# A long convolution by half-size cosine and sine transforms at odd frequencies, in place of full-size ones

## The chip, the cores and the metric

The kernel runs as one program on one core of a Trainium2 chip. The metric is the device time of one execution in microseconds. Five engines take part: TensorE (PE, with its weight loads as PEld), VectorE (DVE), ScalarE (ACT), GpSimd (POOL), and SyncE (SP), whose queue issues the transfers. An instruction waits in its engine's queue until all that it reads and all that it overwrites is ready.

## The reference, cut to what matters

The program is four transformer blocks on 512 tokens of width 1024 with 256 context tokens. The second block's mixer has a long convolution over 512 channels, applied twice, each time followed by a gate:

```python
def two_sided(h_fwd, h_bwd):
    return jnp.concatenate([h_fwd, jnp.zeros((1, h_fwd.shape[1]), h_fwd.dtype), h_bwd[:0:-1]], axis=0)

def fft_long_conv(u, filt2, skip):
    length = u.shape[1]
    n = 2 * length
    y = jnp.fft.irfft(jnp.fft.rfft(u, n=n, axis=1) * jnp.fft.rfft(filt2, n=n, axis=0), n=n, axis=1)[:, :length]
    return y + u * skip.astype(F32)
...
    filt = hyena_filters(length, w1, b1, freq1, w2, b2, freq2, w3)
    z = v
    for order, gate in enumerate((x1, x2)):
        z = gate * fft_long_conv(z, two_sided(filt[:, order, 0], filt[:, order, 1]), skip[order])
```

`hyena_filters` makes the filters from a small network over the 512 positions, times a decay, divided by the sum of their magnitudes. The filters depend on weights alone.

## The kernel before

Every large product is done in split precision: an operand is a rounded high half and the rest, and `mm3` issues three matmuls per tile (lines 90, 91, 92: high x high, data low, weight low). `wsplit` brings a weight tile of 128x512 or 128x1024 by SP's queue, makes its high half on ScalarE (L73, `whi`) and its low half on VectorE (L74, `wlo`); two of each are held. `split` does the same with data (L84, L85). A 128x512 piece of a transform with four tiles of contraction is 12 matmuls of 128x512.

The work of the convolution lies at two places.

The spectra of the two filters are made in the first block's mixer, `even_mixer`. `hyena_spectra` is a generator that `even_mixer` draws on (`next(fg)`) between its own products. The sums and differences of the two filter directions, four tiles each, are split, and the spectrum is made in nine pieces of 128 frequencies x 512 channels (five cosine pieces from the sums, four sine pieces from the differences), each by 12 matmuls with its own 128x512 weight tile. A piece is scaled on VectorE (L713, by the reciprocal norm `hyinv`), the cosine pieces get the skip weight on GpSimd (L715), and SP stores it (L759) from one of two buffers `hyspec`. In the same mixer VectorE does the 31-tap convolution of another branch, 28 taps for each of four channel tiles and two token ranges: 224 instructions of L450. Its gated q, k and v products and the attention follow.

The convolution itself is in the second block's mixer, `odd_mixer`. There the gated delta rule runs in steps (`Delta.step`: `prep`, with a small triangular solve of seven rounds on VectorE at L1183 to L1187, then `recur`), and then `finish`. Each calls `fill()` at its waits, which draws on a generator: first `rows()` (the projections, short convolutions and transposes of the branch, four tiles of v and eight of the gates, steps 2 to 4), then `hyena()`. For each order `hyena` does four frequency tiles: cosine and sine piece (24 matmuls, two weight tiles of 128x512), product with the stored spectrum (`hysp`, L1005, L1006 on VectorE, L1007 on GpSimd), split. Then four token tiles of the inverse, 24 matmuls each with a weight tile of 128x1024, and the gate's multiply (L1022), whose result is split again for the second order. At the end 16 transposes (L1029) bring the result to channels by tokens for the od_w_out product.

The Tile framework's scheduler sets the order on each engine from the order of the program and its pools; each engine then runs its list in order.

## Time and profile before

| | |
|---|---|
| three runs, us | 3699.78, 3704.36, 3707.05 (median 3704.36) |
| profiled execution, us | 3703.5, its span 3701.7 |
| TensorE busy, matmuls | 3475.7 us (94%), 22228 |
| VectorE busy | 2448.4 us (66%) |
| ScalarE, GpSimd busy | 1474.4 us (40%), 683.1 us (18%) |
| DMA | 377.22 MB, mean 102 GB/s |

The profile is that of one execution, on the same core. Busy time is the time in which an engine had an instruction running; matmuls overlap their neighbours, so that the spacing of their starts, and not the duration of one, is what a matmul costs in a row of them. The window view gives busy time per stretch, with the number of instructions in brackets, then the granted TensorE clock as a share of full speed (PEclk), the share of busy DMA engines and the bandwidth. The tile view groups a tile's instructions by line. The timeline view lists single instructions in order of start.

### The profile page before, as it was taken

How to read it: one execution, taken by the hardware profiler on the slowest of the kernel's cores; microseconds unless marked ns; L12 is line 12 of the kernel's file. 1: busy time of each engine (PE TensorE's matmuls, PEld its weight loads, DVE VectorE, ACT ScalarE, POOL GpSimd, SP SyncE). 2: the span in 40 equal slices, each digit the busy share in tenths (PEclk: the TensorE clock that was granted, in tenths of full speed). 3: DMA queues.
4: the chain of work that ended last, by engine and by line, in shares of the span. 5: the costliest groups of instructions: out<-in, count | busy, mean ns of one | idle time of the engine just before them, and what ended most of it. 6: DMA issues, size and time to landing. Idle time of an engine off the chain costs nothing.

```text
span 3701.7 us, 55774 instructions
## 1 busy us (share of the span) xinstructions
PE 3475.7 (94%) x22228; PEld 2869.9 (78%) x22228; DVE 2448.4 (66%) x4099; ACT 1474.4 (40%) x2541; POOL 683.1 (18%) x601
## 2 busy tenths in 40 slices
PE   6898999999998899989999989999999999999999
PEld 4666777888887667667888777767998777767998
DVE  7998877544458765554333776567887676657886
ACT  4213643213226444333223445453443544643443
POOL 0133201002102432221111032022111032011110
PEclk9998999999999999999999989999999999999999
DMA  5244113343333222332232322332333313232333
GB/s 199 80 159 131 49 49 119 115 125 120 119 105 115 84 76 83 120 126 81 91 97 91 111 60 92 108 111 78 105 103 94 122 51 114 80 127 76 106 102 98
DMA packets 161165, 377.22 MB, mean 102 GB/s; under 512 B 19687, under 2 KB 44647, under 8 KB 160520
## 3 DMA queue, kind: packets, MB, share of 16 engines
q1 hardware_dynamic: 160904, 373.65, 32.1%
q8 instruction: 174, 2.85, 0.3%
q14 instruction: 87, 0.71, 0.1%
HBM read 341.61 MB, written 28.84 MB: 100 GB/s over the span
## 4 chain that ended last, share of the span: by engine, by line
PE 40%; DVE 13%; issue 7%; ACT 4%; POOL 2%; DMA 2%; SPq 0%; DVEq 0%; ACTq 0%; POOLq 0%
PE acc L90 11%; PE acc L92 11%; PE acc L91 11%; DVE wlo L74 2%; DMA wraw<-in_w_up_dram 1%; DVE wslo L85 1%; ACT whi L73 1%; DVE hb L1576 1%; PE rec L1301 1%; PE rec L1302 1%; PE rec L1286 1%; DVE ws L1884 1%; DVE xl L1987 1%; DVE oz L819 1%; ACT mp L1811 0%
## 5 line engine op out<-in xcount | busy, mean ns | idle before, releaser
L73 ACT CAST whi<-wraw 128x1024 fp32r<-128x1024 f32 (+2 forms) x468 | 424.0, 906 | 917.9 <-PE acc L91 729.8
L74 DVE TENSOR_TENSOR wlo<-wraw,whi 128x1024 fp32r<-128x1024 f32 (+2 forms) x464 | 511.4, 1103 | 186.0 <-ACT whi L73 181.5
L90 PE MATMUL acc<-hh,whi 128*128 128x512 f32 (+1 forms) x1024 | 366.5, 358 | 11.7 <-ACT whi L73 8.5
L92 PE MATMUL acc<-hh,wlo 128*128 128x512 f32 (+1 forms) x1024 | 363.4, 356 | 10.2 <-POOL wlo L74 5.8
L91 PE MATMUL acc<-hl,whi 128*128 128x512 f32 (+1 forms) x1024 | 364.3, 356 | 1.2 <-DVE hl L256 0.8
L91 PE MATMUL acc<-hidl,whi 128*128 128x512 f32 (+1 forms) x768 | 275.0, 358 | 3.0 <-DVE hidl L85 3.0
L90 PE MATMUL acc<-hidh,whi 128*128 128x512 f32 (+1 forms) x768 | 275.0, 358 | 0.0
L92 PE MATMUL acc<-hidh,wlo 128*128 128x512 f32 (+1 forms) x768 | 274.8, 358 | 0.0
L341 POOL TENSOR_TENSOR sqr<-relu 128x512 f32<-128x512 f32 (+1 forms) x96 | 127.4, 1328 | 688.5 <-ACT relu L339 684.1
L90 PEld LDWEIGHTS acc<-hh,whi 128*128 128x128 f32 x1024 | 195.0, 190 | 51.9 <-ACT whi L73 13.5
L92 PEld LDWEIGHTS acc<-hh,wlo 128*128 128x128 f32 x1024 | 194.0, 190 | 43.9 <-DVE wlo L74 7.7
L91 PEld LDWEIGHTS acc<-hl,whi 128*128 128x128 f32 x1024 | 195.7, 191 | 33.3 <-DVE hl L256 3.5
L92 PE MATMUL acc<-shh,wlo 128*128 128x512 f32 (+1 forms) x480 | 193.7, 404 | 6.7 <-DVE wlo L74 6.7
L90 PE MATMUL acc<-shh,whi 128*128 128x512 f32 (+1 forms) x480 | 195.7, 408 | 3.5 <-ACT whi L73 3.5
L91 PE MATMUL acc<-shl,whi 128*128 128x512 f32 (+1 forms) x480 | 194.2, 405 | 0.0
L85 POOL TENSOR_TENSOR flo<-fth,fhi 128x512 fp32r<-128x512 f32 x44 | 83.7, 1903 | 532.6 <-ACT fhi L84 491.0
L90 PE MATMUL acc<-fsh,wshi 128*128 128x256 f32 x576 | 164.2, 285 | 4.5 <-ACT wshi L84 4.5
L91 PEld LDWEIGHTS acc<-hidl,whi 128*128 128x128 f32 x768 | 145.9, 190 | 26.7 <-DVE hidl L85 3.4
L91 PE MATMUL acc<-fsl,wshi 128*128 128x256 f32 x576 | 163.9, 285 | 0.0
L191 DVE SCALAR_TENSOR_TENSOR mdacc<-wraw,cs,mdacc 128x1024 f32<-128x1024 f32 x70 | 94.4, 1372 | 104.6 <-DMA wraw<-in_ada_w_dram 104.4
L92 PE MATMUL acc<-fsh,wslo 128*128 128x256 f32 x576 | 162.4, 285 | 0.7 <-DVE wslo L85 0.7
L90 PEld LDWEIGHTS acc<-hidh,whi 128*128 128x128 f32 x768 | 144.9, 189 | 23.3
(671 smaller groups left out, 9305.3 us busy)
## 6 DMA issues: line engine op xcount, KB each, us to landing
wraw<-in_mlp_w_dram SPq DMA_DIRECT2D x128, 512.0 KB, 3.5
wraw<-in_ada_w_dram SPq DMA_DIRECT2D x96, 512.0 KB, 4.0
wraw<-in_w_in_dram SPq DMA_DIRECT2D x58, 512.0 KB, 3.5
wraw<-in_od_w_fm_dram SPq DMA_DIRECT2D x36, 512.0 KB, 3.5
wraw<-in_w_gate_dram SPq DMA_DIRECT2D x72, 256.0 KB, 3.2
wraw<-in_w_up_dram SPq DMA_DIRECT2D x72, 256.0 KB, 3.2
wraw<-in_w_down_dram SPq DMA_DIRECT2D x48, 256.0 KB, 2.7
wraw<-in_w_down_dram SPq DMA_DIRECT2D x32, 320.0 KB, 2.9
```

The costliest lines, as they stand in the source:

```text
L73: nc.scalar.copy(hi, raw)
L74: (eng or nc.vector).tensor_tensor(out=lo, in0=raw, in1=f32(hi), op=ALU.subtract)
L85: (eng or nc.vector).tensor_tensor(out=lo, in0=src, in1=f32(hi), op=ALU.subtract)
L90: nc.tensor.matmul(out, s[0], m[0], start=first, stop=False)
L91: nc.tensor.matmul(out, s[0], m[1], start=False, stop=False)
L92: nc.tensor.matmul(out, s[1], m[0], start=False, stop=last)
L191: nc.vector.scalar_tensor_tensor(out=acc, in0=w, scalar=c, in1=acc, op0=ALU.mult, op1=ALU.add)
L341: nc.gpsimd.tensor_tensor(out=s, in0=r, in1=r, op=ALU.mult)
L819: nc.vector.scalar_tensor_tensor(out=o, in0=p[:, j:j + n], scalar=w[:, j:j + 1], in1=o, op0=ALU.mult, op1=ALU.add)
L1286: nc.tensor.matmul(vn_ps[pf[d], hd], wT[:, c, pf[d]], S[:, c], start=True, stop=True)
L1301: nc.tensor.matmul(op_[pf[d], hd], qd[:, c, pf[d]], S[:, c], start=True, stop=False)
L1302: nc.tensor.matmul(op_[pf[d], hd], at[pf[d], c], vn[pf[d], hd], start=False, stop=True)
```

## The change

The transforms are taken at odd frequencies, at which the mirrored tokens around the middle fold into sums and differences of 256 tokens each, for which cosine and sine transforms of half the size do.

- `hyena_spectra`: even and odd lags are transformed apart (the tables of the filter network, `hy_z` and `hy_decay`, are permuted so that tile 0 and 1 hold the even lags). Per parity one weight tile of 128x1024 and two pairs of 6-matmul products; each product is scaled on VectorE (L717 after), the skip is added to the even-lag cosine part on GpSimd, and a sum and a difference on VectorE (L723, L724 after) give two spectrum tiles. 48 matmuls per order, where there were 108; eight stored tiles, where there were nine. `even_mixer` draws on the generator once less per channel tile and range.
- `rows()`: the four v tiles are folded (two half-wide VectorE operations, one input read backwards) before their transposes; of the eight gate tiles the first half is reversed by a ScalarE copy.
- `hyena`: per frequency tile one 128x512 weight tile and 12 matmuls; the inverse makes an even and an odd half for two token tiles, 48 matmuls and two weight tiles of 128x1024 per order; a ScalarE copy of the odd half, a sum and a difference on VectorE give the four token tiles. In order 0 the gated result is folded again before its split. At the end eight transposes become matmuls with the identity read backwards.

```diff
...
                         next(fg, None)
-                        next(fg, None)
                     next(fg, None)
                 for _ in fg:
                     pass
...
     nc.vector.reciprocal(out=inv, in_=acc)
+    nc.scalar.mul(skip, skip, 1.0 / 512)
     yield None
-    for even, pieces in ((True, (0, 1, 2, 3, 8)), (False, (4, 5, 6, 7))):
+    for par in range(2):
         p = []
         for t in range(4):
             s = k.tmp([128, 512], "hys", bufs=2, pool=pool)
-            nc.vector.tensor_tensor(out=s, in0=filt[t], in1=filt[4 + t], op=ALU.add if even else ALU.subtract)
+            nc.vector.tensor_tensor(out=s, in0=filt[t], in1=filt[4 + t], op=ALU.subtract if par else ALU.add)
             hi = k.tmp([128, 512], "hyshi", F32R, 4, pool)
             lo = k.tmp([128, 512], "hyslo", F32R, 4, pool)
             k.split(s, hi, lo)
             p.append((hi, lo))
-        for i in pieces:
-            w = k.wsplit(a["hy_dft"][{4: 8, 8: 9}.get(i, i)], 512)
-            acc = k.tmp([128, 512], "acc", pool=ps, bufs=None)
-            for t in range(4):
-                s = slice(t * 128, t * 128 + 128)
-                k.mm3(acc, (w[0][:, s], w[1][:, s]), p[t], t == 0, t == 3)
-            o = k.tmp([128, 512], "hyspec", bufs=2, pool=pool)
-            nc.vector.tensor_tensor(out=o, in0=acc, in1=inv, op=ALU.mult)
-            if even:
-                nc.gpsimd.tensor_tensor(out=o, in0=o, in1=skip, op=ALU.add)
-            yield i, o
+        w = k.wsplit(a["hy_lag"][par])
+        for i in range(2):
+            eo = []
+            for odd in range(2):
+                acc = k.tmp([128, 512], "acc", pool=ps, bufs=None)
+                for t in range(2):
+                    c = odd * 512 + t * 256 + i * 128
+                    k.mm3(acc, (w[0][:, c:c + 128], w[1][:, c:c + 128]), p[2 * odd + t], t == 0, t == 1)
+                o = k.tmp([128, 512], "hys", bufs=2, pool=pool)
+                nc.vector.scalar_tensor_tensor(out=o, in0=acc, scalar=1.0 / 512, in1=inv, op0=ALU.mult, op1=ALU.mult)
+                eo.append(o)
+            e, o = eo
+            lo_, hi_ = (k.tmp([128, 512], "hyspec", bufs=2, pool=pool) for _ in range(2))
+            if par == 0:
+                nc.gpsimd.tensor_tensor(out=e, in0=e, in1=skip, op=ALU.add)
+            nc.vector.tensor_tensor(out=lo_, in0=o, in1=e, op=ALU.add)
+            nc.vector.tensor_tensor(out=hi_, in0=o if par else e, in1=e if par else o, op=ALU.subtract)
+            yield (4 * par + i, lo_), (4 * par + 2 + i, hi_)
 def hyena_filters(k, ps, pool):
...
-            if it:
-                nc.sync.dma_start(out=k.spec[o, it[0]], in_=it[1])
+            for n, t in it or ():
+                nc.sync.dma_start(out=k.spec[o, n], in_=t)
             yield
...
                 w = k.wsplit(a["od_w_fm"][i])
                 z = conv(pp, acc, T, hyw[:, i], 3, hyb[:, i:i + 1])
-                tp = transposed(z, 4)
+                if i < 4:
+                    sd = k.tmp([128, 512], "otm", bufs=2, pool=pp)
+                    for j, op in enumerate((ALU.add, ALU.subtract)):
+                        nc.vector.tensor_tensor(out=sd[:, 256 * j:256 * j + 256], in0=z[:, 256:], in1=z[:, 255::-1], op=op)
+                    tp = transposed(sd, 4)
+                else:
+                    zr = k.tmp([128, 512], "otm", bufs=2, pool=pp)[:, :256]
+                    nc.scalar.copy(zr, z[:, 255::-1])
+                    tp = TP()
+                    for t, src in enumerate((z[:, 256:384], z[:, 384:], zr[:, :128], zr[:, 128:])):
+                        nc.tensor.transpose(tp[:, t * 128:(t + 1) * 128], src, k.ident)
...
 def hyena(k, u, xg, spec, ps, pool, ps1):
-            for j in (i, 4 + i) + ((8,) if i == 0 else ()):
+            for j in (i, 4 + i):
                 t = k.tmp([128, 512], "hysp", bufs=3, pool=pool)
                 nc.sync.dma_start(out=t, in_=spec[order, j])
                 sp.append(t)
-            A, B, A2 = sp[0], sp[1], sp[-1] if i == 0 else sp[0]
+            A, B = sp
             f = []
-            for j in (i, 4 + i):
-                w = k.wsplit(a["hy_dft"][j], 512)
+            w = k.wsplit(a["hy_dft"][i], 512)
+            for j, v in enumerate((u[:2], u[2:])):
                 acc = k.tmp([128, 512], "prep" if order and i % 2 else "acc", pool=ps1 if order and i % 2 else ps, bufs=None)
-                for t in range(4):
-                    s = slice(t * 128, t * 128 + 128)
-                    k.mm3(acc, (w[0][:, s], w[1][:, s]), (u[t][:, 0], u[t][:, 1]), t == 0, t == 3)
+                for t in range(2):
+                    s = slice(j * 256 + t * 128, j * 256 + t * 128 + 128)
+                    k.mm3(acc, (w[0][:, s], w[1][:, s]), (v[t][:, 0], v[t][:, 1]), t == 0, t == 1)
                 f.append(acc)
             yield
-            for j, (p, q, op) in enumerate(((A, B, ALU.subtract), (B, A2, ALU.add))):
+            for j, (p, q, op) in enumerate(((A, B, ALU.subtract), (B, A, ALU.add))):
                 t1 = k.tmp([128, 512], "hyt1", bufs=2, pool=pool)
                 t2 = k.tmp([128, 512], "hyt2", bufs=2, pool=pool)
                 nc.vector.tensor_tensor(out=t1, in0=f[0], in1=p, op=ALU.mult)
...
                 lo = k.tmp([128, 512], "hyyl", F32R, 8, pool)
                 k.split(t1, hi, lo)
                 ys[i + 4 * j] = (hi, lo)
-        z = []
-        for t in range(4):
+        z = [None] * 4
+        for t in range(2):
+            g = [k.tmp([128, 512], "hyg", bufs=4, pool=pool) for _ in range(2)]
+            for i in range(2):
+                nc.sync.dma_start(out=g[i], in_=xg[order, t + 2 * i])
+            eo = []
             w = k.wsplit(a["hy_idft"][t])
-            g = k.tmp([128, 512], "hyg", bufs=2 if order == 0 else 4, pool=pool) if order == 0 else k.tmp([128, 512], "hysp2", bufs=4, pool=pool)
-            nc.sync.dma_start(out=g, in_=xg[order, t])
-            acc = k.tmp([128, 512], "acc", pool=ps, bufs=None)
-            for j in (0, 4, 1, 5, 2, 6, 3, 7):
-                s = slice(j * 128, j * 128 + 128)
-                k.mm3(acc, (w[0][:, s], w[1][:, s]), ys[j], j == 0, j == 7)
-            yield
-            nc.vector.tensor_tensor(out=g, in0=acc, in1=g, op=ALU.mult)
+            for j in range(2):
+                acc = k.tmp([128, 512], "acc", pool=ps, bufs=None)
+                for i in range(4):
+                    s = slice(j * 512 + i * 128, j * 512 + i * 128 + 128)
+                    k.mm3(acc, (w[0][:, s], w[1][:, s]), ys[4 * j + i], i == 0, i == 3)
+                eo.append(acc)
+                yield
+            o = k.tmp([128, 512], "hyt2", bufs=2, pool=pool)
+            nc.scalar.copy(o, eo[1])
+            for i in range(2):
+                v = k.tmp([128, 512], "hyt1", bufs=2, pool=pool)
+                nc.vector.tensor_tensor(out=v, in0=eo[0], in1=o, op=ALU.subtract if i else ALU.add)
+                nc.vector.tensor_tensor(out=g[i], in0=v, in1=g[i], op=ALU.mult)
+                z[t + 2 * i] = g[i]
             if order == 0:
-                k.split(g, u[t][:, 0], u[t][:, 1])
-            z.append(g)
+                for i in range(2):
+                    v = k.tmp([128, 512], "hyt1", bufs=2, pool=pool)
+                    nc.vector.tensor_tensor(out=v, in0=g[0], in1=g[1], op=ALU.subtract if i else ALU.add)
+                    k.split(v, u[t + 2 * i][:, 0], u[t + 2 * i][:, 1])
     for c in range(4):
         tp = k.tmp([128, 512], "acc", pool=ps, bufs=None)
-        for t in range(4):
-            nc.tensor.transpose(tp[:, t * 128:(t + 1) * 128], z[t][:, c * 128:(c + 1) * 128], k.ident)
+        s = slice(c * 128, (c + 1) * 128)
+        for t in range(2):
+            nc.tensor.matmul(tp[:, (1 - t) * 128:(2 - t) * 128], z[2 + t][:, s], k.ident[:, ::-1], start=True, stop=True)
+            nc.tensor.transpose(tp[:, (2 + t) * 128:(3 + t) * 128], z[t][:, s], k.ident)
         k.split(tp, u[c][:, 0], u[c][:, 1])
...
-        k.spec = k.dram.tile([2, 9, 128, 512], F32, name="spec")
+        k.spec = k.dram.tile([2, 8, 128, 512], F32, name="spec")
...
+    perm = np.concatenate([t[::2], t[1::2]])
...
+    c["hy_lag"] = np.stack([np.concatenate([side(tab(fn, 2 * q + o)) for o in range(2)], axis=1) for fn in (np.cos, np.sin)]).astype(f)
+    cos, sin = (fn(math.pi * (((2 * q[None, :] + 1) * (2 * q[:, None] + 1)) % 4096) / 2048) for fn in (np.cos, np.sin))
...
```

The scheduler's lists change with it. First VectorE's list in the even mixer, where the first spectrum tiles are made, taps among them. Before (`hyspec` is a spectrum piece, `conv` a tap's output):

```order
L409 TENSOR_REDUCE lams<-c_ev_lam 128x2
L450 SCALAR_TENSOR_TENSOR conv_112<-xl_504,c_ev_conv_w,conv_112 128x512 x2
L713 TENSOR_TENSOR hyspec_632<-acc_619,hyinv_587 128x512
L411 TENSOR_SCALAR lam<-lams 128x1
L420 SCALAR_TENSOR_TENSOR xl_504<-th_661,acc_663 128x256
L74 TENSOR_TENSOR wlo_693<-wraw_690,whi_692 128x512
L421 TENSOR_SCALAR conv_112<-xl_504,c_ev_conv_w,c_ev_conv_b 128x256
L74 TENSOR_TENSOR wlo_716<-wraw_713,whi_715 128x512
L450 SCALAR_TENSOR_TENSOR conv_112<-xl_504,c_ev_conv_w,conv_112 128x512
L450 SCALAR_TENSOR_TENSOR conv_112<-xl_504,c_ev_conv_w,conv_112 128x256
L450 SCALAR_TENSOR_TENSOR conv_112<-xl_504,c_ev_conv_w,conv_112 128x512
L713 TENSOR_TENSOR hyspec_709<-acc_696,hyinv_587 128x512
```

After (`hys` is a scaled even or odd part, L449 a tap, L74 a weight's low half):

```order
L74 TENSOR_TENSOR wlo_727<-wraw_724,whi_726 128x1024
L717 SCALAR_TENSOR_TENSOR hys_681<-acc_674,hyinv_587 128x512
L411 TENSOR_SCALAR lam<-lams 128x1
L717 SCALAR_TENSOR_TENSOR hys_690<-acc_683,hyinv_587 128x512
L449 SCALAR_TENSOR_TENSOR conv_112<-xl_504,c_ev_conv_w,conv_112 128x512
L723 TENSOR_TENSOR hyspec_692<-hys_690,hys_681 128x512
L724 TENSOR_TENSOR hyspec_693<-hys_681,hys_690 128x512
L449 SCALAR_TENSOR_TENSOR conv_112<-xl_504,c_ev_conv_w,conv_112 128x512
L717 SCALAR_TENSOR_TENSOR hys_706<-acc_699,hyinv_587 128x512
L717 SCALAR_TENSOR_TENSOR hys_715<-acc_708,hyinv_587 128x512
L74 TENSOR_TENSOR wlo_733<-wraw_730,whi_732 128x1024
```

The sum of L723 and the difference of L724 stand behind both scaled parts, and the first parts' skip add lies on GpSimd between them; the next pair follows a tap later.

VectorE's list around the low halves of the V product's weights (L74; `conv_115` is the last channel tile's taps). Before:

```order
L161 TENSOR_TENSOR mods_3_2043<-acc_2467,c_ada_b 128x16
L450 SCALAR_TENSOR_TENSOR conv_115<-xl_504,c_ev_conv_w,conv_115 128x256
L74 TENSOR_TENSOR wlo_2476<-wraw_2473,whi_2475 128x1024
L450 SCALAR_TENSOR_TENSOR conv_115<-xl_504,c_ev_conv_w,conv_115 128x256
L462 TENSOR_TENSOR cv_451_2573<-conv_112,conv_113 128x512
L450 SCALAR_TENSOR_TENSOR conv_115<-xl_504,c_ev_conv_w,conv_115 128x256
L462 TENSOR_TENSOR cv_451_2573<-cv_451_2573,conv_114 128x512
L450 SCALAR_TENSOR_TENSOR conv_115<-xl_504,c_ev_conv_w,conv_115 128x256
```

After:

```order
L161 TENSOR_TENSOR mods_3_1859<-acc_2283,c_ada_b 128x16
L449 SCALAR_TENSOR_TENSOR conv_115<-xl_504,c_ev_conv_w,conv_115 128x256
L74 TENSOR_TENSOR wlo_2292<-wraw_2289,whi_2291 128x1024
L449 SCALAR_TENSOR_TENSOR conv_115<-xl_504,c_ev_conv_w,conv_115 128x256
L74 TENSOR_TENSOR wlo_2308<-wraw_2305,whi_2307 128x1024
L449 SCALAR_TENSOR_TENSOR conv_115<-xl_504,c_ev_conv_w,conv_115 128x256
L461 TENSOR_TENSOR cv_421_2389<-conv_112,conv_113 128x512
L449 SCALAR_TENSOR_TENSOR conv_115<-xl_504,c_ev_conv_w,conv_115 128x256
```

207 taps stand ahead of the first of these low halves before and 212 ahead of the second, which is not shown; after, 214 and 215.

VectorE's list in the odd mixer's step 5, at the end of the seven rounds of the solve (`T8`, `sh`; `Tm` is their result). Before:

```order
L1183 STREAM_SHUFFLE sh_2417_13939<-T8_2411_13907 128x32 x2
L1184 TENSOR_TENSOR sh_2417_13939<-sh_2417_13939,Lc_2410_13905 128x32 x2
L1185 TENSOR_TENSOR T8_2411_13907<-T8_2411_13907,sh_2417_13939 128x64
L1183 STREAM_SHUFFLE sh_2418_13945<-T8_2411_13907 128x32 x2
L1184 TENSOR_TENSOR sh_2418_13945<-sh_2418_13945,Lc_2410_13905 128x32 x2
L1185 TENSOR_TENSOR T8_2411_13907<-T8_2411_13907,sh_2418_13945 128x64
L1187 TENSOR_TENSOR Tm_2419_13951<-T8_2411_13907,c_dn_m8_10040 128x256
L1022 TENSOR_TENSOR hyg_2456_14114<-acc_2457_14116,hyg_2456_14114 128x512
L1189 STREAM_TRANSPOSE R_2420_13953<-Tm_2419_13951 128x256
L74 TENSOR_TENSOR wlo_2474_14305<-wraw_2472_14302,whi_2473_14304 128x1024
L85 TENSOR_TENSOR hyv0_9458<-hyg_2456_14114,hyv0_9458 128x512
```

After (the rounds are L1219 to L1221, `Tm` is L1223):

```order
L1221 TENSOR_TENSOR T8_2383_13695<-T8_2383_13695,sh_2389_13727 128x64
L74 TENSOR_TENSOR wlo_2498_14306<-wraw_2496_14303,whi_2497_14305 128x512
L1219 STREAM_SHUFFLE sh_2390_13733<-T8_2383_13695 128x32 x2
L1052 TENSOR_TENSOR hyt1_2439_14038<-acc_2427_13888,hyt2_2438_14036 128x512
L1220 TENSOR_TENSOR sh_2390_13733<-sh_2390_13733,Lc_2382_13693 128x32 x2
L1053 TENSOR_TENSOR hyg_2422_13878<-hyt1_2439_14038,hyg_2422_13878 128x512
L1221 TENSOR_TENSOR T8_2383_13695<-T8_2383_13695,sh_2390_13733 128x64
L1052 TENSOR_TENSOR hyt1_2440_14041<-acc_2427_13888,hyt2_2438_14036 128x512
L1223 TENSOR_TENSOR Tm_2391_13739<-T8_2383_13695,c_dn_m8_9856 128x256
L1053 TENSOR_TENSOR hyg_2423_13879<-hyt1_2440_14041,hyg_2423_13879 128x512
L1225 STREAM_TRANSPOSE R_2392_13741<-Tm_2391_13739 128x256
L1058 TENSOR_TENSOR hyt1_2441_14044<-hyg_2422_13878,hyg_2423_13879 128x512
```

Before, the first result of the inverse (`hyg`, L1022) stands behind the last round; after, a sum of the inverse's halves (L1052) stands ahead of the last round's multiply, and its difference ahead of `Tm`.

## Rows read from the trace of the kernel before

**Rows 1.** Page, section 1: engine, busy us, share, instructions.

```profile
...
PE 3475.7 (94%) x22228; PEld 2869.9 (78%) x22228; DVE 2448.4 (66%) x4099; ACT 1474.4 (40%) x2541; POOL 683.1 (18%) x601
...
```

**Rows 2.** Windows, even mixer; the first line names the columns.

```profile
...
core 0: us, PE busy (x) PEld busy (x) DVE busy (x) ACT busy (x) POOL busy (x), PEclk, DMA share, GB/s
60.00:345.00 285.00, 245.19 (x1266) 191.30 (x1266) 274.60 (x417) 80.62 (x128) 81.73 (x49) 0.93 0.37 117
345.00:375.00 30.00, 28.29 (x202) 23.53 (x199) 12.98 (x35) 12.95 (x26) 3.94 (x5) 0.95 0.42 142
...
```

**Rows 3.** Windows, odd mixer: steps 2 to 5 and the finish; columns as above.

```profile
...
1304.00:1360.00 56.00, 51.83 (x591) 37.82 (x590) 32.12 (x90) 21.07 (x46) 20.95 (x30) 1.00 0.27 86
1360.00:1432.00 72.00, 68.49 (x657) 49.88 (x656) 39.26 (x105) 30.83 (x63) 20.82 (x39) 0.98 0.26 78
1432.00:1502.00 70.00, 68.36 (x659) 49.09 (x658) 44.20 (x104) 27.56 (x53) 23.37 (x36) 1.00 0.37 114
1502.00:1587.00 85.00, 77.69 (x689) 54.09 (x687) 47.19 (x108) 21.93 (x40) 21.19 (x23) 0.96 0.26 81
1587.00:1650.00 63.00, 53.91 (x225) 41.39 (x225) 43.50 (x61) 23.74 (x61) 17.18 (x13) 0.90 0.41 132
...
```

**Rows 4.** Lines, VectorE, 60 to 345 us: busy us, mean ns | idle before.

```profile
...
L450 DVE SCALAR_TENSOR_TENSOR conv<-xl,c_ev_conv_w,conv 128x512 f32<-128x512 f32 (+1 forms) x224 | 149.9, 726 | 0.1
...
L713 DVE TENSOR_TENSOR hyspec<-acc,hyinv 128x512 f32<-128x512 f32 x18 | 12.3, 685 | 2.1 <-issue 1.6 <-PE acc L92 0.4
...
```

**Rows 5.** Tile hyspec: count, ns min/median/max, first and last start.

```profile
...
L715 POOL TENSOR_TENSOR hyspec<-hyspec,hyskip x10: 1275/1672/3475, 86.6 to 201.4; 128x512 f32<-128x512 f32 x10
...
DMA to landing us min/median/max: 2.0/2.1/4.7
```

**Rows 6.** Tile hyshi, the same columns.

```profile
...
L90 PE MATMUL acc<-hyshi,whi x72: 388/399/792, 81.3 to 214.3; 128*128 128x512 f32 x72
...
L84 ACT CAST hyshi<-hys x16: 602/620/629, 45.3 to 203.7; 128x512 fp32r<-128x512 f32 x16
L85 DVE TENSOR_TENSOR hyslo<-hys,hyshi x16: 627/688/1773, 46.4 to 204.7; 128x512 fp32r<-128x512 f32 x16
...
```

**Rows 7.** Timeline, TensorE, finish: start, us, line, operation.

```profile
...
1621.63 0.39 PE L92 MATMUL acc<-hyyh,wlo 128*128 128x512 f32 x1
...
1622.33 0.39 PE L92 MATMUL acc<-hyyh,wlo 128*128 128x512 f32 x1
...
```

**Rows 8.** Timeline, VectorE, end of the taps; in brackets the idle time before.

```profile
...
314.99 2.83 DVE L74 TENSOR_TENSOR wlo<-wraw,whi 128x1024 fp32r<-128x1024 f32 x1
...
339.15 0.92 DVE L450 SCALAR_TENSOR_TENSOR conv<-xl,c_ev_conv_w,conv 128x256 f32<-128x256 f32 x1
...
369.83 0.16 DVE L107 TENSOR_SCALAR ms<-acc 128x2 f32<-128x2 f32 x1 [10.55 <-PE acc L103]
...
```

**Rows 9.** Timeline, VectorE, step 2.

```profile
...
1314.50 0.41 DVE L1185 TENSOR_TENSOR T<-T,sh 128x64 f32<-128x64 f32 x1
...
1315.65 1.22 DVE L74 TENSOR_TENSOR wlo<-wraw,whi 128x1024 fp32r<-128x1024 f32 x1
...
1324.30 0.43 DVE L1187 TENSOR_TENSOR Tm<-T,c_dn_m 128x256 f32<-128x256 f32 x1
...
```

**Rows 10.** Timeline, VectorE, step 5.

```profile
...
1516.88 0.69 DVE L74 TENSOR_TENSOR wlo<-wraw,whi 128x512 fp32r<-128x512 f32 x1
...
1518.55 0.21 DVE L1185 TENSOR_TENSOR T<-T,sh 128x64 f32<-128x64 f32 x1
...
1534.60 0.43 DVE L1187 TENSOR_TENSOR Tm<-T,c_dn_m 128x256 f32<-128x256 f32 x1
...
```

**Rows 11.** Tile hysp (spectra, gates): count, ns min/median/max, starts.

```profile
...
L1029 PE MATMUL acc<-c_ident,hysp x16: 270/273/329, 1643.8 to 1647.1; 128*128 128x128 f32 x16
L1005 DVE TENSOR_TENSOR hyt<-acc,hysp x12: 676/686/693, 1481.8 to 1610.8; 128x512 f32<-128x512 f32 x12
...
L1022 DVE TENSOR_TENSOR hysp<-acc,hysp x4: 692/692/692, 1626.3 to 1644.0; 128x512 f32<-128x512 f32 x4
...
```

27 lines of the change are left out of this document (12 added, 15 removed).

## The prediction

> **What bounds the kernel now.** I read the page's busy shares first, then the windows over the two places that the change touches, then single tiles and timelines there. TensorE is busy 94% of the span [rows 1], so by the whole-span view every matmul less is time won, and the change takes 312 of 22228 away. But the share is a mean, and the two places differ.
>
> Place A is the even mixer from 60 to 345 us, where the filter spectra are made. There VectorE is busy 274.6 of 285 us and TensorE 245.2 [rows 2]. What fills VectorE is the 31-tap convolution: 224 taps of 0.726 us, with an idle time of 0.1 us before all of them together [rows 4]. They are wanted before the attention, and the last one starts at 339.15 [rows 8]. VectorE sets the end of A. Once the taps are done, TensorE does: at 369.83 VectorE has stood 10.55 us for the accumulator of L103 [rows 8], and TensorE is busy 28.3 of 30 us from 345 to 375 [rows 2].
>
> Place B is the odd mixer's chunk steps and finish, 1304 to 1650 us. TensorE is busy 51.8 of 56, 68.5 of 72, 68.4 of 70, 77.7 of 85 and 53.9 of 63 us in steps 2 to 5 and the finish; VectorE is between 55 and 69% [rows 3]. The long convolution runs as filler at the end of step 4, in step 5 and in the finish. TensorE sets the end of B.
>
> Everything from the od_w_out product on keeps its order of instructions on every engine, and so does what lies between A and B; what the two places give is handed on whole.
>
> **The price of a matmul.** Two rows of L92 in the inverse transform are three matmuls apart and start at 1621.63 and 1622.33 [rows 7]: 0.70/3 = 0.233 us per 128x512 matmul. The duration that a row shows, 0.39, is longer, since neighbours overlap.
>
> **Place B, part by part.** Forward: per order 96 matmuls become 48. Inverse: again 96 become 48. Two orders: 384 - 192 = 192 fewer, 192 x 0.233 = 44.7 us of TensorE.
>
> VectorE in B: per order eight lo halves of 128x512 and four of 128x1024 become four and two, so 4 x 0.69 [rows 10] and 2 x 1.22 [rows 9] = 5.2 us go. Added per order: four sums that read an accumulator (0.692, as L1022 [rows 11]), 2.8 us, and in order 0 four more sums at 0.688 [rows 6], 2.8 us. In all 10.4 go and 8.3 come. ScalarE gets two copies per order of 0.62 [rows 6] and loses half of its hi halves. SP's queue loses half of the weight bytes and one spectrum tile per order. All this lies beside TensorE and I count it at nothing; VectorE's slack in step 5, 85 - 47.2 = 37.8 us [rows 3], is the cover.
>
> Two things come onto the path. First the tail: before, one multiply of 0.692 stands between the last inverse matmul and the first transposes of L1029 [rows 11]. After, it is the copy of the odd half 0.62, sum, multiply, difference, multiply: 0.62 + 2 x 0.692 + 2 x 0.688 = 3.38, so +2.7. Between order 0 and order 1 the same chain stands with two more sums, but step 5's own matmuls are there to hide it: 0 taken, 4.1 if not. Second the rows stage: four pairs of half-wide sums, each pair like one 128x512 operation of 0.688, and eight half-wide copies on ScalarE at half of 0.62: 2.8 + 2.5 = 5.2 us if all of it is waited for. No row shows a reversed read, so its speed is open. TensorE has other work in these steps (95% busy in step 3 [rows 3]), so I take 2, with 0 and 5.2 as the ends.
>
> B = -44.7 + 2.7 + 2.0 = -40.0. The low end: the seven rounds of the small triangular solve take 9.8 us in step 2 (1314.50 to 1324.30 [rows 9]) and 16.05 us in step 5 (1518.55 to 1534.60 [rows 10]), where the convolution's operations stand between the rounds. If the stretch of 6.3 us goes as well: -44.7 - 6.3 = -51. The high end is the first rival's.
>
> **Place A, part by part.** Per order 108 matmuls become 48, so 120 x 0.233 = 28.0 us of TensorE go. They lie beside the taps and count nothing as long as VectorE ends last. So I count VectorE: 18 multiplies (0.685 [rows 4]) and 18 lo halves (0.69) go, 24.75 us; four lo halves of 1.22, 16 scaled multiplies of accumulators at 0.685 and 16 sums or differences at 0.688 come, 26.85 us. That is +2.1.
>
> The skip adds on GpSimd fall from 10 to 4. A VectorE subtract that reads two SBUF tiles takes 0.688 at the median and 1.773 at most [rows 6]; I read the 1.085 us between them as the price of meeting a GpSimd operation. Six fewer: -6.5. The Trainium skill (SBUF — State Buffer, "Who interferes with whom") says that the pair of ports which VectorE and GpSimd share is an exclusive lock, and that the loser stands still for the whole instruction; by that rule the six adds of 1.67 us would give back up to 10 us, and A would be 3.5 us lower than by the row. I keep the row, whose longest instruction is 1.773.
>
> New waits: in the even pairs VectorE's first sum, L723, stands in order behind the skip add. That add takes 1.672 us at the median, 3.475 at most [rows 5]; VectorE has one multiply and one tap in between, 0.685 + 0.726 = 1.41, so it waits 0.3 to 2.1 us, with the taps queued behind. I take 1, four times: +4. The two spectrum buffers are stored and reused: landing takes 2.1 us [rows 5], and between one pair's sums and the next one's stand a tap, two multiplies and a lo half, 0.726 + 1.37 + 1.22 = 3.3 us. 0 taken; the last rival has the price.
>
> The lo half of the first V weight, which starts at 314.99 [rows 8], stands behind 207 taps before and 214 now; the second moves only from 212 to 215. TensorE's V product and the attention wait for them: 0 to 7 x 0.726 = 5.1 us, I take half, +2.5.
>
> A = 2.1 - 6.5 + 4 + 2.5 = +2.1.
>
> **The sum.** The profiled execution takes 3703.5 us, 1.8 around its span, and 0.9 below the median of 3704.4. 3703.5 - 40.0 + 2.1 = 3665.6; against the median 3666.5. I predict 3666, with a range of its own from 3652 to 3678.
>
> **Rivals.**
>
> *The forward transform becomes VectorE's.* Per frequency tile TensorE falls from 24 x 0.233 = 5.6 to 2.8 us, while VectorE keeps four multiplies (0.686 [rows 11]), two lo halves (0.688) and one weight's lo half (0.69): 4.8 us. If the forward runs at that pace, its four tiles take 19.2 instead of 22.4 us, so each order's forward gives 3.2 us and not 11.2. Then B = -22.4 (inverses) - 6.4 + 4.7 = -24.1 and the time 3682; if step 5 also ends by its solve and order 0 gives nothing, B is about -17.7 and the time 3689. For it: in the new order the last rounds of the solve stand behind the inverse's results on VectorE, and the inverse's matmuls stand ahead of the solve's next products on TensorE. Against: order 1's first two tiles now lie inside step 5, where VectorE has those 37.8 us.
>
> *A gains too.* If the V product, and not the taps, set A's end all along, the 28.0 us are won there: 3704.4 - 40 - 28 = 3636. For it: the wait of 10.55 us on TensorE after the last tap. Against: 274.6 of 285 us, and the V weights' lo halves are themselves queued behind the taps.
>
> *The clock eats it.* The clock granted in the finish is 0.90 of full [rows 3], so part of it ran at the lower of the two levels, 1.2 of 2.4 GHz; a matmul there takes 0.792 us against 0.399 [rows 6]. With half of the matmuls gone the chains between them stay, and TensorE stands idle more. If order 1's 96 remaining matmuls all run at the lower level, 22.4 us come back: 3689. The Trainium skill (TensorE: Matmul & The Clock Gate, "HAM oscillation — how this bites in real kernels") tells of a kernel in which idle gaps between short bursts send the clock down each time, so that each burst starts cold. The trace agrees that the lower level appears where TensorE has gaps; that the gaps grow so far isn't shown.
>
> *Slower: VectorE stands at L723.* In eight pairs it would wait for the stores of the pair before (4.7 us at the longest) and in the four even ones for the skip add as well (3.475): 4 x 8.2 + 4 x 4.7 = 51.5 us on the engine that bounds A, in place of the 4 taken: 3714. It decides from 49 us, 6.2 per pair. Against: both are the longest single values of their rows, and the median landing fits into the 3.3 us between.
>
> **How the numbers follow.** Forecast 0.55, the forward on VectorE 0.20, A too 0.10, the clock 0.10, slower 0.05. 0.2% is 7.4 us, about what a measurement of this kernel can tell. The slower case is the only one over it; the same-time band (3697 to 3712) is reached only where the first and third rival, or small stalls of the last, come together: 0.05. Faster gets 0.90. The range goes from 3644, part of the way into the second rival, to 3692, which takes in the first and third.
>
> **What would show it.** In A: VectorE still over 95% busy to its last tap, that tap within some 5 us of 339, TensorE with some 28 us less; if the tap's end or the attention moves early by over 10 us, my A is wrong. In B: step 5 and finish together some 40 us shorter, most of it TensorE's busy time; a TensorE share there that falls well below 85% with VectorE near 90% is the first rival, a granted clock near 0.6 in the finish the third. Waits of L723 over 5 us each are the last. A tail of about 3.4 us from the last inverse matmul to the transposes is the term of 2.7. The forecast is wrong if the time is above 3692 or below 3644.

## The result, and the profile after

The changed kernel takes 3668.27 us (median of four runs, 3667.19 to 3674.40), the kernel before 3702.07 (four runs, 3693.39 to 3707.05): the medians differ by 33.8 us. The ratio of the runs is 0.9915, 95% interval 0.9892 to 0.9937: 0.85% faster. 3666 was predicted, from 3644 to 3692. The profiled spans, from which all that follows is read, differ by 36.3 us.

The total is close; its terms are not. The page's first lines after, then the windows over A (columns as in [rows 2]):

```profile
span 3665.4 us, 55031 instructions
...
PE 3410.3 (93%) x21924; PEld 2813.6 (77%) x21924; DVE 2439.1 (67%) x4107; ACT 1464.3 (40%) x2529; POOL 680.0 (19%) x595
...
```

```profile
...
60.00:345.00 285.00, 227.34 (x1177) 176.26 (x1178) 272.13 (x425) 72.50 (x114) 80.37 (x44) 0.86 0.36 115
345.00:375.00 30.00, 27.27 (x181) 23.53 (x180) 17.43 (x40) 19.67 (x38) 2.94 (x4) 0.87 0.23 70
...
```

TensorE's records are 304 fewer [rows 1], where the prediction takes 312 away, as each of the eight matmuls with the reversed identity appears as two. Against [rows 2] TensorE is busy 17.9 us less in A, where 28.0 were worked out (the granted clock of the window fell from 0.93 to 0.86), VectorE 2.5 us less, and VectorE is still at 95%. The windows over B, cut at the end of step 4, at the end of the solve and at the end of step 5:

```profile
...
1428.50:1503.00 74.50, 72.73 (x691) 50.46 (x689) 45.42 (x107) 31.14 (x61) 26.86 (x40) 1.00 0.34 104
1503.00:1530.00 27.00, 19.58 (x66) 13.03 (x66) 26.38 (x74) 6.35 (x10) 12.08 (x12) 0.81 0.35 97
1530.00:1573.20 43.20, 37.43 (x513) 26.02 (x513) 23.53 (x43) 13.00 (x28) 8.43 (x9) 0.96 0.26 81
1573.20:1622.00 48.80, 33.62 (x119) 24.74 (x120) 34.26 (x47) 16.69 (x51) 14.41 (x11) 0.76 0.29 95
...
```

From step 4 to the od_w_out product it was 218 us, 200.0 of them busy on TensorE (68.36, 77.69 and 53.91 in [rows 3]); now 193.5, of them 163.4. TensorE's work shrank by 36.6 us, and its idle time grew from 18.0 to 30.1. And the granted clock is 0.81 in the solve's window and 0.76 in the finish. VectorE is busy 26.38 of 27 us in the solve.

To compare kernels I cut every trace at three instructions that all of them have: the start of the first row maximum of the attention (mx<-S), the start of the solve's reduction in step 4 (Lc<-LM), the start of the first residual add behind the od_w_out product (xl<-acc,mods,xl). The stretches are differences of these rows' starts, in us:

| kernel | to attention | to step 4's solve | B | rest |
|---|---|---|---|---|
| before | 375.5 | 1064.4 | 219.1 | 2042.7 |
| changed | 368.3 | 1068.1 | 196.4 | 2032.6 |
| spectra only | 365.1 | 1071.1 | 219.4 | 2040.6 |
| convolution only | 375.6 | 1065.3 | 197.5 | 2037.3 |
| half of the spectra's matmuls | 375.9 | 1077.9 | 218.3 | 2048.0 |
| half of the convolution's matmuls | 373.6 | 1068.0 | 198.4 | 2040.2 |
| no skip adds | 363.7 | 1069.2 | 219.1 | 2043.5 |
| transposes last | 367.9 | 1067.9 | 190.6 | 2036.0 |
| norm at once | 368.6 | 1070.8 | 189.8 | 2036.9 |
| idle filled | 369.6 | 1068.3 | 196.4 | 2043.8 |
| no low halves | 366.8 | 1071.7 | 189.7 | 2034.0 |
| skip at lag zero | 370.8 | 1065.8 | 189.0 | 2035.5 |
| changed again | 367.7 | 1074.5 | 202.9 | 2033.1 |

So A gave 7.2 us, B 22.7; the stretch between lost 3.7, and the rest, with the same instructions in the same order, gave 10.1. Most of the rows stage lies in the stretch between; its share is 0.9 (from step 2's solve to step 4's it is 128.2 us, and 127.3 before). One trace per kernel is little, but the groups don't overlap: with the spectra of before the attention starts at 373.6 to 375.9 (apart from the kernel without skip adds), with the new ones at 365.1 to 370.8; B takes 218.3 to 219.4 us with the convolution of before at full work, 196.4 to 202.9 with the changed one at full work, and 189.0 to 190.6 with the changed one and the transposes last.

### The profile page after: what moved, and what is told of

Same layout as the page of the kernel before. It is cut to its first block, busy times and chain, and to the rows that moved or that the text cites. A ratio compares the mean times of both kernels' runs of the same rounds, so it can differ in the third digit from the quotient of the medians.

```text
span 3665.4 us, 55031 instructions
## 1 busy us (share of the span) xinstructions
PE 3410.3 (93%) x21924; PEld 2813.6 (77%) x21924; DVE 2439.1 (67%) x4107; ACT 1464.3 (40%) x2529; POOL 680.0 (19%) x595
## 4 chain that ended last, share of the span: by engine, by line
PE 39%; DVE 14%; issue 7%; ACT 4%; POOL 2%; DMA 2%; SPq 0%; DVEq 0%; POOLq 0%; ACTq 0%
PE acc L90 11%; PE acc L92 11%; PE acc L91 10%; DVE wlo L74 2%; DMA wraw<-in_w_up_dram 2%; DVE wslo L85 1%; DVE hb L1612 1%; ACT whi L73 1%; PE rec L1337 1%; PE rec L1338 1%; DVE ws L1920 1%; PE rec L1322 1%; DVE oz L828 1%; ACT mp L1847 0%; DVE xl L2023 0%
## 5 line engine op out<-in xcount | busy, mean ns | idle before, releaser
L73 ACT CAST whi<-wraw 128x1024 fp32r<-128x1024 f32 (+2 forms) x442 | 408.0, 924 | 843.3 <-PE acc L91 652.9
L74 DVE TENSOR_TENSOR wlo<-wraw,whi 128x1024 fp32r<-128x1024 f32 (+2 forms) x438 | 490.5, 1120 | 184.7 <-ACT whi L73 180.5
L90 PEld LDWEIGHTS acc<-hidh,whi 128*128 128x128 f32 x768 | 144.8, 188 | 23.5
L92 PEld LDWEIGHTS acc<-hidh,wlo 128*128 128x128 f32 x768 | 144.8, 189 | 23.2
```

The source lines that it names most:

```text
L73: nc.scalar.copy(hi, raw)
L74: (eng or nc.vector).tensor_tensor(out=lo, in0=raw, in1=f32(hi), op=ALU.subtract)
L90: nc.tensor.matmul(out, s[0], m[0], start=first, stop=False)
L92: nc.tensor.matmul(out, s[1], m[0], start=False, stop=last)
```

## The experiments

**Each place alone.** The spectra alone (the odd mixer's code as before), and the convolution with its rows alone (the spectra's code as before):

```diff
-                nc.sync.dma_start(out=t, in_=spec[order, j])
+                nc.sync.dma_start(out=t, in_=spec[order, j % 8])
```

is the spectra-only kernel's edit to the convolution of before (its ninth tile isn't there), and

```diff
-            w = k.wsplit(a["hy_dft"][{4: 8, 8: 9}.get(i, i)], 512)
+            w = k.wsplit(a["hy_dftf"][{4: 8, 8: 9}.get(i, i)], 512)
```

the convolution-only kernel's to the spectra of before (the full-size table under another name).

> The new spectra of stage A alone; the odd mixer's rows and long convolution as before, at full size (it multiplies with spectra of another transform, and reads eight tiles where it read nine, so the output is not the reference's). Theory 1, the working of the prediction: VectorE bounds A, the time moves by about +2 us (-3 to +6). Theory 2, fewer GpSimd adds free VectorE by more than the row told: about -6 us, as the attention of the changed kernel starts 5.9 us earlier in its trace. Rival, TensorE bounds A: -28 us.

Measured: 3700.27 against 3704.82 us, ratio 0.9987 (0.9978 to 0.9995), -4.6 us; the attention starts 10.4 us earlier, and the stretch behind it loses 6.7 of them again.

> The new rows stage and half-size long convolution alone; the spectra are made as before, at full size (so the output is not the reference's). Theory 1, TensorE bounds B: -40 us. Theory 2, read from the two traces: VectorE paces the forward transform in step 5's solve, and the norm of the finish holds TensorE's queue: -22 to -28 us, with the od_w_out product starting some 22 us earlier.

Measured: 3676.97 against 3704.82, ratio 0.9925 (0.9910 to 0.9940), -27.9 us; B is 21.6 us shorter. Both times that fits theory 2. The parts sum to -32.4; the whole measured -33.8.

**Fewer matmuls and nothing else.** The kernel before, with half of the matmuls left out in one place: in the spectra by the first edit, in the second kernel in hyena's forward by the same one and in its inverse by the other (the flag that ends an accumulation moves to the last matmul that is left):

```diff
-                for t in range(4):
+                for t in range(2):
...
-            for j in (0, 4, 1, 5, 2, 6, 3, 7):
+            for j in (0, 4, 1, 5):
```

> The kernel before with half of the spectra's matmuls left out (two of four contraction tiles, 108 fewer, 25 us of TensorE); everything else of A as before. VectorE bounds A: 0 (-3 to +3). TensorE bounds A: -25 us.

Measured: the attention starts at 375.9, as before (375.5). 25 us of TensorE's work are worth nothing in A. VectorE bounds it, as predicted. Yet the run as a whole took 3719.15 us, ratio 1.0038 (1.0024 to 1.0053): neither theory has that. The table puts it into the two stretches that nobody touched (+13.5 and +5.3 us); more on that in the last section.

> The kernel before with half of the long convolution's matmuls left out (two of four contraction tiles forward, four of eight inverse: 192 fewer, as the change has them); no operation is added, so no tail, no folding, and all weights' halves are still made. Theory 1, TensorE bounds B: -44.7 us, solve of step 5 shorter than its 16 us. Theory 2, VectorE and the finish's norm bound it: -20 to -30 us, the solve of step 5 not shorter than in the trace before, the granted clock in the finish below 0.85.

Measured: 3676.77 us, ratio 0.9932 (0.9915 to 0.9948), -28.1; B is 20.7 us shorter, not 44.7. So taking the matmuls out, without the folding and the tail, gives no more than the change does. The solve's first and last row in step 5:

```profile
...
1516.38 0.59 DVE L1175 TENSOR_REDUCE Lc<-LM 128x64 f32<-128x256 f32 x1
...
1539.83 0.42 DVE L1187 TENSOR_TENSOR Tm<-T,c_dn_m 128x256 f32<-128x256 f32 x1
...
```

23.5 us from the reduction to Tm. Before it was 18.3, from this row to 1534.60 [rows 10]:

```profile
...
1516.32 0.64 DVE L1175 TENSOR_REDUCE Lc<-LM 128x64 f32<-128x256 f32 x1
...
```

With the change it is 21.5:

```profile
...
1508.27 0.59 DVE L1211 TENSOR_REDUCE Lc<-LM 128x64 f32<-128x256 f32 x1
...
1529.82 0.41 DVE L1223 TENSOR_TENSOR Tm<-T,c_dn_m 128x256 f32<-128x256 f32 x1
...
```

So with half of the matmuls the solve gets no shorter. What TensorE waits for from there on in the kernel with half of the matmuls (who waits, for whom, us in all, times, longest; `wlo` is a weight's low half, `xl` at L1325 a normalised tile of the finish, `hyt` a product with the spectrum):

```profile
...
PE acc L92 <- DVE wlo L74: 9.6, 4, 2.8
PE prep L1332 <- DVE xl L1325: 5.8, 3, 2.9
PE acc L90 <- DVE hyt L1006: 3.0, 1, 3.0
...
```

All of these wait for VectorE; the whole list comes to 28.8 us, 26.3 of them for VectorE and 2.5 for ScalarE. The granted clock of the finish (1587.3 to 1628 us) is 0.79. Theory 1 is out for B.

**GpSimd's adds.** The kernel before without the line that adds the skip:

```diff
-            if even:
-                nc.gpsimd.tensor_tensor(out=o, in0=o, in1=skip, op=ALU.add)
```

> The kernel before without the ten skip adds on GpSimd (the skip term is left out of the result). Theory 2, GpSimd's operations slow VectorE in stage A: the last tap ends and the attention starts some 10 us earlier than before (10 adds at 1.085 us by the prediction's row, more if the row is too small). If they don't matter: within 2 us.

Measured: the last tap ends at 326.9 instead of 340.1, the attention starts 11.8 us earlier; the whole took 3697.13 us in its one run, against a median of 3702.70. VectorE's taps, weights' low halves, rotary operation, data's low halves and filter sums (columns as in [rows 4]), first without the adds:

```profile
...
L450 DVE SCALAR_TENSOR_TENSOR conv<-xl,c_ev_conv_w,conv 128x512 f32<-128x512 f32 (+1 forms) x224 | 145.1, 704 | 0.1
L74 DVE TENSOR_TENSOR wlo<-wraw,whi 128x512 fp32r<-128x512 f32 (+1 forms) x33 | 32.7, 990 | 1.1 <-ACT whi L73 1.1
...
L496 DVE TENSOR_TENSOR rt<-rt,c_rope2d 128x512 f32<-128x512 f32 x8 | 9.6, 1205 | 0.0
...
L85 DVE TENSOR_TENSOR hyslo<-hys,hyshi 128x512 fp32r<-128x512 f32 x12 | 7.9, 684 | 1.7 <-ACT hyshi L84 1.7
L701 DVE TENSOR_TENSOR hys<-hyf,hyf 128x512 f32<-128x512 f32 x10 | 6.4, 679 | 0.0
...
```

Before, where the taps' mean was 726 [rows 4]:

```profile
...
L74 DVE TENSOR_TENSOR wlo<-wraw,whi 128x512 fp32r<-128x512 f32 (+1 forms) x33 | 34.5, 1044 | 2.5 <-ACT whi L73 2.5
...
L85 DVE TENSOR_TENSOR hyslo<-hys,hyshi 128x512 fp32r<-128x512 f32 x12 | 10.0, 865 | 2.4 <-ACT hyshi L84 2.4
L496 DVE TENSOR_TENSOR rt<-rt,c_rope2d 128x512 f32<-128x512 f32 x8 | 9.6, 1202 | 0.0
...
L701 DVE TENSOR_TENSOR hys<-hyf,hyf 128x512 f32<-128x512 f32 x10 | 7.5, 792 | 0.0
...
```

By the counts that is 4.9 + 1.8 + 2.2 + 1.1 = 10.0 us, 1.0 per add, near the row's 1.085; the rest of the 13.1 us is idle time of VectorE, in these rows and in L713's (2.1 [rows 4], now 0.7). The rotary operation keeps its mean, which will matter below. The Trainium skill (SBUF — State Buffer, "Who interferes with whom") has the loser blocked for the whole of the other instruction, which, as an estimate from 1.67 us, would be up to 16.7 for ten adds. The measured 10.0 stays below that without contradicting it, as one meeting in the kernel before shows: the add runs from 92.16 to 93.83 us, its first 0.52 us beside a low half on VectorE (92.00 to 92.68) that is not lengthened, and the tap behind that one takes 1.78 us, 1.04 more than the 0.74 of others of its shape.

**The finish's queue.** The changed kernel, with the finish's transposes behind all filler; then also (the lines on t, ss and r) with one norm for all tiles, after all squares:

```diff
-        for hd in range(H):
-            fill()
+        for _ in range(6):
+            fill()
+        for hd in range(H):
...
-        for t in range(4):
+        for t in (1, 2, 0, 3):
...
-            nc.vector.tensor_scalar(out=ss[:, t], in0=ss[:, t], scalar1=1.0 / 128, scalar2=EPS, op0=ALU.mult, op1=ALU.add)
-            nc.gpsimd.tensor_tensor(out=r[:, t], in0=ss[:, t], in1=k.mhalf[:, :H], op=ALU.pow)
+        nc.vector.tensor_scalar(out=ss, in0=ss, scalar1=1.0 / 128, scalar2=EPS, op0=ALU.mult, op1=ALU.add)
+        nc.gpsimd.tensor_tensor(out=r, in0=ss, in1=k.mhalf[:, :4 * H].rearrange("p (t h) -> p t h", t=4), op=ALU.pow)
```

What TensorE waits for from step 5's solve on in the changed kernel (columns as above):

```profile
...
PE prep L1368 <- DVE xl L1361: 8.0, 3, 4.5
PE acc L90 <- DVE hyt L1027: 5.0, 2, 4.7
PE acc L92 <- DVE wlo L74: 4.5, 2, 3.1
...
```

L1368 are the finish's transposes. They wait for L1361, which multiplies by GpSimd's power, and stand ahead of the rest of the convolution's matmuls. Before, the same transposes (L1332) waited less, and for the convolution's product, not for the norm:

```profile
...
PE prep L1332 <- DVE hyt L1005: 4.2, 2, 2.8
...
```

> The changed kernel, with the 16 transposes of the finish put behind all filler, so that TensorE's queue meets the convolution's matmuls first. Theory 2, the transposes that wait for the finish's norm hold TensorE: the od_w_out product starts 5 to 12 us earlier than in the changed kernel, and less of the finish runs at the lower clock. Theory 1, they are hidden: within 2 us.

Measured: B is 5.8 us shorter than in the changed kernel (190.6), as theory 2 has it, and the granted clock from 1573 to 1616 us is 0.84; 3665.37 us, ratio to before 0.9897 (0.9883 to 0.9911). With the next run's that is the lowest ratio, though the interval overlaps the change's.

> As the run before, and the norm of the finish is made for all four token tiles by one VectorE and one GpSimd instruction instead of four pairs in turn. Theory 2: again 2 to 5 us earlier, since the norm's hops between VectorE and GpSimd no longer stand between the forward transform's operations. If VectorE's own work and not the hops bounds the finish: within 2 us of the run before.

Measured: B 189.8, 0.8 us less than the run before: 2 to 5 were expected, so the norm's hops are not what is left (the run without low halves, below, points to VectorE's own work). The whole took 3667.52 us, ratio 0.9898 (0.9884 to 0.9912).

**The clock.** The changed kernel with idle places filled:

```diff
+                for _ in range(((16, 5, 8, 4), (0, 0, 0, 0), (0, 0, 0, 0), (10, 0, 0, 0))[hd][t]):
+                    nc.tensor.matmul(tp[:, t * 128:(t + 1) * 128], k.ident, k.ident, start=True, stop=True)
                 nc.tensor.transpose(tp[:, t * 128:(t + 1) * 128], oacc[:, t, hd], k.ident)
```

What it is about, in the changed kernel's timeline of TensorE:

```profile
...
1575.96 0.39 PE L92 MATMUL acc<-hyv,wlo 128*128 128x512 f32 x1
1580.86 0.47 PE L1368 MATMUL prep<-c_ident,xl 128*128 128x128 f32 x1 [4.50 <-DVE xl L1361]
...
1581.56 0.63 PE L91 MATMUL prep<-hyv,whi 128*128 128x512 f32 x1
1581.98 0.63 PE L92 MATMUL prep<-hyv,wlo 128*128 128x512 f32 x1
...
```

After a wait of 4.50 us a matmul takes 0.63, and the next one starts after 0.42 to 0.43 us, not 0.233: the lower level (the granted clock from 1580.9 to 1584 us is 0.50).

> The changed kernel with 43 matmuls of the identity by itself put into the places of the finish at which TensorE waits for the norm; their results are overwritten. If the lower clock after these waits is what the finish lost (the third rival): granted clock in the finish above 0.9 instead of 0.76, and the od_w_out product starts 4 to 8 us earlier. If the waits alone are the loss: 0 to 3 us later.

Measured, the finish with the matmuls added:

```profile
...
1578.00:1626.00 48.00, 39.15 (x206) 32.16 (x205) 35.20 (x49) 18.10 (x53) 14.44 (x11) 0.89 0.30 97
...
```

The granted clock rises from 0.76 to 0.89, and B takes 196.4 us as without them; the finish itself is 1.8 us shorter (56.4 against 58.2 from the last row of step 5 to the residual add), and what came before it took as much more. The Trainium skill (TensorE: Matmul & The Clock Gate, "HAM oscillation — how this bites in real kernels") tells of gaps that bring the lower level each time; the trace agrees (0.50 behind the wait of 4.50 us). But here filling the gaps won 1.8 us in the finish and nothing in B: most of what TensorE does slowly it would otherwise wait for. As the added matmuls take time too, that is a rough price of the clock. The run as a whole took 3682.96 us, ratio 0.9943 (0.9930 to 0.9956), 14.7 us more than the changed kernel, and again the table has most of the difference in the rest (+11.2).

**VectorE's work.** The changed kernel without order 0's low halves:

```diff
-                lo = k.tmp([128, 512], "hyyl", F32R, 8, pool)
-                k.split(t1, hi, lo)
+                if order == 0:
+                    nc.scalar.copy(hi, t1)
+                    lo = hi
+                else:
+                    lo = k.tmp([128, 512], "hyyl", F32R, 8, pool)
+                    k.split(t1, hi, lo)
```

> The changed kernel, in order 0 without the eight low halves of the products with the spectrum (the high half is used in their place, so that TensorE's matmuls stay as many): 8 x 0.69 = 5.5 us less for VectorE between step 4 and step 5. Theory 2, VectorE paces the convolution there: step 5 ends 3 to 6 us earlier than in the changed kernel, counted from the start of step 3. If TensorE paces it: within 1 us.

Measured: from step 4's solve to the end of step 5 135.3 us against 138.1, 2.8 us less where 3 to 6 were expected; the solve takes 19.6 us, where the six other kernels with this convolution and these spectra have 21.5 to 21.9. With as many matmuls, 5.5 us less for VectorE shortened the solve by 2 us: VectorE paces it. B is 189.7 against 196.4, but one trace doesn't tell such a difference from chance (the changed kernel's own two differ by 6.5, below). The run as a whole, its only one, took 3664.03 us.

**The last adds.** The transposes-last kernel with the skip at lag zero:

```diff
-    nc.scalar.mul(skip, skip, 1.0 / 512)
+    nc.vector.tensor_tensor(out=skip[0:1], in0=acc[0:1], in1=skip[0:1], op=ALU.mult)
+    nc.vector.tensor_tensor(out=filt[0][0:1], in0=filt[0][0:1], in1=skip[0:1], op=ALU.add)
...
-            if par == 0:
-                nc.gpsimd.tensor_tensor(out=e, in0=e, in1=skip, op=ALU.add)
```

> The run with the transposes last, and the skip weight is added to the filter at lag zero (two VectorE operations on one partition per order) instead of to the spectrum (two GpSimd adds of 128x512 per order). Theory 2, each GpSimd add costs VectorE over 1 us in stage A: the attention starts 3 to 6 us earlier than in the changed kernel, and the od_w_out product 10 to 13 us earlier. If the remaining four adds cost nothing: the attention within 2 us.

Measured: a miss. The attention starts at 370.8, 2.5 us later than in the changed kernel; the first tap starts at 90.4 where it was 85.9, so from the first tap to the attention it takes 2.0 us less. There was little to win: in the changed kernel's trace the four adds lengthen one tap (1.275 us at 85.89) and two weights' low halves (2.005 at 90.70, 1.844 at 172.60), against 0.74 and 1.22 otherwise, by 1.9 us in all. And the taps' mean is 724 ns, not 707, though no skip add is left: the lists shifted, and the four longest taps (2.57 to 2.90 us) each overlap one of the weights' low halves that GpSimd makes; in the changed kernel three do. 3671.98 us, ratio 0.9915 (0.9900 to 0.9929).

**The same again.**

> The changed kernel once more, to see how far one execution's stretches repeat. If the lower-clock intervals in the untouched stretches belong to the kernel, its stretches repeat within 2 us; if they belong to the execution, stretches of the same instructions differ by 2 to 5 us, in steps that go with the intervals.

Measured: 3680.00 us in its one run, against 3667.19 to 3674.40. From attention to step 4's solve it took 1074.5 against 1068.1, B 202.9 against 196.4. Of the 6.5 us in B, 5.3 are one stretch, the same 691 matmuls:

```profile
...
1434.30:1514.10 79.80, 77.21 (x691) 52.59 (x689) 46.07 (x107) 31.14 (x61) 26.42 (x40) 0.94 0.31 97
...
```

79.8 us at a granted clock of 0.94, where the changed kernel's first trace had 74.5 at 1.00. So some of the intervals belong to the execution, and with them some of every comparison made here. Not all: the kernel with half of the spectra's matmuls was slower in each of its six runs (3711.23 at least) than the kernel before in any of eighteen beside it (3709.98 at most).

## Why the prediction was right, and where it was not

**Bounds.** That VectorE bounds A was right (half of the spectra's matmuls: 0.4 us). That TensorE bounds B was wrong for the solve of step 5 and for the finish.

**The price of a matmul** held at the full clock: from 1611.76 to 1612.47 us, rows below, three take 0.71. TensorE's work in B shrank by 36.6 us where 44.7 were worked out; at the lower level, of which the solve and the finish now hold more (granted clocks of 0.81 and 0.76), one takes up to 0.43.

**Place B**: -40.0 was forecast, -22.7 measured. The step that failed is "All this lies beside TensorE and I count it at nothing; VectorE's slack in step 5 [...] is the cover". The 37.8 us were a total over step 5. The slack lies behind the solve; in the solve, where the convolution's VectorE operations run, there was none even before:

```profile
...
1511.10:1534.60 23.50, 17.77 (x62) 12.82 (x62) 23.25 (x70) 5.72 (x8) 10.06 (x10) 0.88 0.48 148
...
```

VectorE busy 23.25 of 23.5 us, and now 26.38 of 27. So the solve grew from 18.3 to 21.5 us. In the finish the norm's chain came into the open: TensorE's queue stands 8.0 us at the transposes that wait for it, and putting them last made B 5.8 us shorter. The first rival had both the place (VectorE takes over) and the size, -24.1; its second price, -17.7, is what comes out if neither order's forward gives anything (6.4 us), while its words name order 0 alone. The low end of the range for B, a shorter solve, had the wrong sign. The third rival's lower clock came (0.90 to 0.76 in the finish), its price did not: 22.4 us were reckoned, and filling the gaps won 1.8 in the finish.

The tail, forecast at +2.7, is +3.7: from the last inverse matmul to the first od_w_out matmul it took 4.35 us before,

```profile
...
1643.53 0.39 PE L92 MATMUL acc<-hyyh,wlo 128*128 128x512 f32 x1
...
1647.88 0.50 PE L90 MATMUL acc<-hyv,whi 128*128 128x512 f32 x1 [0.54 <-DVE hyv L85]
...
```

and now 8.10:

```profile
...
1611.76 0.40 PE L92 MATMUL acc<-hyyh,wlo 128*128 128x512 f32 x1
...
1612.47 0.39 PE L92 MATMUL acc<-hyyh,wlo 128*128 128x512 f32 x1
...
1620.57 0.48 PE L90 MATMUL acc<-hyv,whi 128*128 128x512 f32 x1
...
```

The rows stage, forecast at +2, is +0.9.

**Place A**: +2.1 was forecast, -7.2 measured. The wait at L723 never came:

```profile
...
L449 DVE SCALAR_TENSOR_TENSOR conv<-xl,c_ev_conv_w,conv 128x256 f32<-128x256 f32 (+1 forms) x224 | 145.6, 707 | 0.1
...
L85 DVE TENSOR_TENSOR hyslo<-hys,hyshi 128x512 fp32r<-128x512 f32 x12 | 7.7, 684 | 1.5 <-ACT hyshi L84 1.5
...
L495 DVE TENSOR_TENSOR rt<-rt,c_rope2d 128x512 f32<-128x512 f32 x8 | 6.5, 821 | 0.0
L723 DVE TENSOR_TENSOR hyspec<-hys,hys 128x512 f32<-128x512 f32 x8 | 6.0, 751 | 0.0
...
```

Its idle time is 0.0 where +4 was taken: the four adds took 1.29, 1.30, 2.18 and 1.29 us, and each had ended before VectorE came to L723.

The V product came earlier, not later, where +2.5 was taken: the low half of its first weight starts at 312.54, where it was 314.99 [rows 8].

The six adds fewer were sized about right: the taps' mean fell from 726 to 707 ns, hyslo's from 865 to 684 and the filter sums' (L701, now L703) from 792 to 682, which is 4.3 + 2.2 + 1.3 = 7.8 us where 6.5 were taken (the two runs on the adds agree: 10.0 us for ten, of which 1.9 are left with four).

The rotary operation's mean fell from 1202 to 821, 3.0 us that no term had. That isn't the adds' doing, since it is 1205 without any of them; before, three of its eight instructions take 1.61 to 2.84 us and overlap GpSimd's weight low halves, and with the shifted lists none does.

On the other side the weights' low halves on VectorE shrank by 5.7 us (34.5 to 28.8 in the two views) where 18 x 0.69 - 4 x 1.22 = 7.5 were worked out.

Together that is 4 + 2.5 + 1.3 + 3.0 - 1.8 = 9.0 of the 9.3 us between forecast and measurement; the sum is read from rows, and no run takes it apart. The last tap's end moved from 340.1 to 330.8:

```profile
...
312.54 2.82 DVE L74 TENSOR_TENSOR wlo<-wraw,whi 128x1024 fp32r<-128x1024 f32 x1
...
329.77 1.00 DVE L449 SCALAR_TENSOR_TENSOR conv<-xl,c_ev_conv_w,conv 128x256 f32<-128x256 f32 x2
...
361.69 0.16 DVE L107 TENSOR_SCALAR ms<-acc 128x2 f32<-128x2 f32 x1 [6.23 <-PE acc L103]
...
368.27 0.96 DVE L574 TENSOR_REDUCE mx<-S 128x1 f32<-128x768 f32 x1 [0.67 <-PE S L571]
...
```

The second rival (28 us) is out, and the last one too: its waits are not there.

**The rest**: 0 was forecast, -10.1 measured (below). In all: B gave 17.3 us less than forecast, A 9.3 more, and 6.4 came from what was not touched. That these cancel, and the total lies 2 us from the forecast, is luck.

## What to carry to other kernels

Read the slack of an engine in the very stretch in which the added or remaining work will stand, not over the step that holds it: here 47.19 busy us of 85 hid 23.25 of 23.5 where it mattered. When matmuls go, ask what they covered: here a normalisation chain and its transposes, queued ahead of the next product, took the place, and putting them last was worth 6 us in that stretch. When instructions on one engine go, look at which of the others' operations now meet: here a change of GpSimd's and VectorE's lists alone moved single operations by 1 to 2 us. Where a change is worth 1%, cut the traces at instructions that both kernels share, since stretches that hardly changed moved by up to 13.5 us.
